# Block inverse read from PSUM at its first turn and turned in storage order at its end, with a replanned order of issue

## The chip, the cores and the metric

One core of one Trainium2 chip runs the whole kernel. The metric is the device time of one execution in microseconds (us). Before the change the median of three executions was 1673.81 us (1667.06 to 1674.06).

## The reference, cut to what matters

The kernel computes two layers on 768 tokens (one sequence of 512, one of 256): a Mamba-2 layer in both directions, then an RWKV-7 layer in both directions, each followed by a residual and a layer norm. The change touches the RWKV-7 recurrence, which for each of 16 heads of 64 channels is

```
def step(s, inp):
    r_t, w_t, k_t, v_t, kk_t, a_t = inp
    sa = einsum('bhvk,bhk->bhv', s, -kk_t)
    s = s * w_t[:, :, None, :] + sa[..., None] * (kk_t * a_t)[:, :, None, :] + v_t[..., None] * k_t[:, :, None, :]
    return s, einsum('bhvk,bhk->bhv', s, r_t)
```

The state s feeds its own update. Taken 64 tokens at a time, all the updates of one chunk solve a unit lower triangular system, and the kernel inverts its 64 by 64 matrix.

## The kernel before, in words

**Stages.** In the Mamba-2 part (0 to about 770 us of the trace) large matmuls, each split into three float32r products (lines 140 to 142), fill TensorE. The RWKV-7 part (from about 770 us) goes over eight blocks b of 128 channels, two heads each. For a block, `rwkv_in` projects and stores the inputs, `p1` prepares six windows of four 64-token chunks, `rwkv_inverse` inverts the 24 units (chunks of both directions), and eight calls of `chain_step` run the recurrence. `rwkv_final` normalises the output. A ring of 32 slots (`slot`, line 697) holds the matrices G, TD and BK of 24 units and of 8 of the next block, so that windows of block b+1 fill slots that steps of block b have freed.

**The windows.** `p1_back` computes a window's matrices into the PSUM tile `ptd` (line 899), which lies in the one buffer of bank tag "s", and VectorE masks them into TD (line 901) and G (line 904, two halves). The last of these reads frees bank "s".

**The inverse.** TD holds a 64 by 64 matrix a unit and head. The two diagonal blocks of 32 by 32 are blended into the SBUF tile TC, laid out as (unit, row), first by ScalarE (line 936) and then by VectorE (line 937), for the first 16 units and then for the other 8. The first turn (line 942, a VectorE transpose of 128x1024) reads TC with the unit innermost, a stride of 32 elements, and writes TS in storage order. Here `sw` swaps the two free dimensions. ScalarE copies TS to the PSUM tile TL, which is taken from bank "s" (line 943); VectorE sets its diagonal (line 944) and solves 30 columns in place, two operations a column (lines 949 and 950). Two turns bring the result to SBUF, both writing at a stride of 32 elements:

```
TL = self.pt("s", [P, 32, 32], "tl")
nc.vector.transpose(TS, sw(TC))
...
nc.vector.transpose(sw(XN), sw(TL))
XR = TC
nc.vector.transpose(sw(XR), TL)
```

The second turn of the end (line 954) reads TL in storage order, the first (line 952) at a stride. Then TL is written again, by matmuls of 32x32 (line 963, TD by XN), so these wait until the turn of line 954 has read it. ScalarE scales the product into E (line 965) and writes XR back to TD (line 968, two operations for each group of units). A second set of 32x32 matmuls (line 972, E by XR) goes to a new tile px, and VectorE and ScalarE copy it to TD (line 975). The steps of the next block wait for that.

**The order of issue.** No order is written by hand. `arrange` (line 1841) gives the whole program to `Program`, whose `estimate` (line 1343) sets the cost of every instruction. `schedule` (line 1768) runs a list scheduler (`forward`, line 1545) under three sets of parameters with eight passes each; `timing` (line 1732) plays every order on a model of the engines (`Machine`, line 1783), and the order with the earliest end becomes a chain of dependences on every engine. SP issues all DMAs, in that order too. In the model a DMA lands DMA_NS = 1700 ns (line 1236) plus its bytes at 250 bytes a ns after its issue, one after another. Three estimates matter later: a VectorE operation of N elements costs (66 + N)/0.96 ns whatever its strides, so a turn is put at 1135 ns; a DMA has no cost for the size of its pieces; and a matmul of another tile size than the one before waits for TURN = 95 ns (line 1240) after the array has drained.

Of the kernel before, what the change touches and what calls it, by code (L numbers as in the profile page):

```python
# [58 lines left out]
class Trunk:  # L59
# [507 lines left out]
    def rwkv(self):  # L567
        nc, d = self.nc, self.d
        with ExitStack() as cx:
# [52 lines left out]
            self.Y = keep(rw, "Y", [NCH, 2, C])  # L622
            ri = self.pool("ri", 1, ctx=tail)
            self.TC, self.TL, self.XN = (keep(ri, n, [32, 32]) for n in ("TC", "TL", "XN"))
            nc.gpsimd.memset(self.TC, 0.0)
            prep = tail.enter_context(ExitStack())
            rp = self.rp = self.pool("rp", 1, ctx=prep)
            self.lora()
# [299 lines left out]
    def rwkv_inverse(self, b):  # L928


        nc = self.nc
        TD, TC, TS, XN = self.TD, self.TC, self.TL, self.XN
        hm = self.halfm
        spans = [(slice(u, u + n), slice(o, o + n)) for u, o, n in self.spans(b)]
        for us, rs in spans:
            nc.scalar.activation(TC[:, us], TD[:, rs, 0, 0:32], AF.Copy, scale=hm[:, 2:3])
            nc.vector.scalar_tensor_tensor(TC[:, us], TD[:, rs, 0, 32:64], hm[:, 3:4], TC[:, us], op0=ALU.mult, op1=ALU.add)
        fl = lambda t: t.rearrange("p a b -> p (a b)")
        sw = lambda t: t.rearrange("p a b -> p b a")

        TL = self.pt("s", [P, 32, 32], "tl")
        nc.vector.transpose(TS, sw(TC))
        nc.scalar.copy(TL, TS)
        nc.vector.memset(fl(TL)[:, ::33], 1.0)
        tmp = fl(XN)
        for j in range(1, 31):
            m = 31 - j
            t = tmp[:, 0 : m * j].rearrange("p (a b) -> p a b", b=j)
            nc.vector.tensor_tensor(t, bc(TS[:, j + 1 : 32, j], 2, j), bc(TL[:, j, 0:j], 1, m), op=ALU.mult)
            nc.vector.tensor_add(TL[:, j + 1 : 32, 0:j], TL[:, j + 1 : 32, 0:j], t)  # L950

        nc.vector.transpose(sw(XN), sw(TL))
        XR = TC
        nc.vector.transpose(sw(XR), TL)
        qs = [(slice(64 * h, 64 * h + 32), slice(64 * h + 32, 64 * h + 64)) for h in range(2)]
        E = TS
        groups = (slice(0, 16), slice(16, 24))
        place = [o + i for _, o, n in self.spans(b) for i in range(n)]
        ps = TL
        for g in groups:  # L960
            for u in range(24)[g]:
                for q0, q1 in qs:
                    nc.tensor.matmul(ps[q1, u, :], TD[q0, place[u], 0, 32:64], XN[q0, u, :], start=True, stop=True)
# [272 lines left out]
DMA_NS = 1700  # L1236
TICK = 10240 / 3
WARM = 2900
SPAN = 3400
TURN = 95.0  # L1240

DRAIN = {"Activation": 122.0, "DVE": 90.0}
FULL = (128, 128)
# [4 lines left out]
        self.keep, self.stay, self.pace, self.spare = keep, stay, pace, spare  # L1248


PASSES = 8
PARAMS = Params(4000, 1000, 1.6, 2.3), Params(6000, 1000, 1.6, 2.0), Params(5000, 2000, 1.6, 2.6)


def size(ap, first=1):
# [24 lines left out]
    return p0 // 32, (p0 + pn + 31) // 32, bits << lo  # L1280


def in_dram(ap):
    lo = int(ap.offset)
    hi = lo + sum((int(n) - 1) * abs(int(s)) for s, n in ap.ap)
    a, z = lo // 4096, hi // 4096
    return 0, 1, ((1 << (z - a + 1)) - 1) << a
# [6 lines left out]
class Program:  # L1294


    def __init__(self, nc, tc):
        self.ins = ins = list(nc.cur_bb.bb.instructions)
        n = len(ins)
        self.eng = [str(x.engine).split(".")[-1] for x in ins]  # L1300
        self.pred = [set() for _ in ins]
        self.cost, self.dma, self.cols = [0.0] * n, [0.0] * n, [0.0] * n
        self.cells, self.kind = [()] * n, [1] * n
        self.mode, self.lock = [FULL] * n, [0.0] * n
        self.part = [None] * n
        self.after, self.rationed = defaultdict(set), set()
        self.raw = set()
        aps, self.acc = [], defaultdict(list)
        for i, x in enumerate(ins):
            io = [[a.bass_ap for a in l if getattr(a, "bass_ap", None) is not None] for l in (x.ins, x.outs)]  # L1310
            aps.append(io)
            for b in io[0] + io[1]:
                if hasattr(b.tensor, "cap_key"):
                    self.acc[b.tensor.name].append(i)
            if io[0] or io[1]:
                self.estimate(i, x, *io)
        self.trace(nc, tc, aps)
        self.classify()
# [24 lines left out]
    def estimate(self, i, x, src, dst):  # L1343
        e, op = self.eng[i], x.opcode
        if e == "SP":
            dram = src and dst and any(hasattr(a.tensor, "cap_key") and space(a.tensor, "DRAM") for a in src + dst)
            self.cost[i] = 1.0 if not dst else 560.0 if dram else 400.0
            if dst:
                self.dma[i] = size(dst[0], 0) * 4 / 250.0
            return  # L1350
        if e == "PE":
            N, M, K = size(src[0]), size(src[1]), int(src[0].ap[0][1])
# [4 lines left out]
            if x.is_transpose:  # L1357
                self.cost[i] = 2 * max(N, M) / 2.4 + 2.5
                self.cols[i] = 2 * N * K / 128
                return  # L1360
            self.mode[i] = up(K), up(M)
            if not f32:
                r = str(x.ins[0].dtype) == "dt.float32r"
                self.cost[i] = N / (2.226 if r else 2.4) + 2.0
                self.cols[i] = N * K / 128
                if N >= 256:
                    self.kind[i] = 2
                    if r and M <= 64:
                        self.mode[i] = FULL
                return  # L1370
# [3 lines left out]
            self.cost[i] = cyc / 2.4 + 2.5  # L1374
            self.cols[i] = (2 if M <= 64 else 4) * N * K / 128
            if M <= 64:
                self.cost[i] = max(N, 64) / 64 * 108.0
                if N < 64:
                    self.cost[i] = 93.0
                self.kind[i] = 0  # L1380
            return
        N = max(size(a) for a in src + dst)
# [6 lines left out]
        if e == "DVE":  # L1389
            if op != "TensorScalarPtr":  # L1390
                c = (66 + N) / 0.96
                if op == "Reciprocal":
                    c = 70 + N * 6.4
            elif x.ins and two == 1 and not ps:
                c = 69 + N / 1.92 + 61 * ptr
            else:
                c = (66 + N) / 0.96 + 61 * ptr
            if getattr(x, "is_tensor_tensor_scan", False):
                c = 70 + 2.07 * N
            if not ps and N > 16:  # L1400
# [4 lines left out]
        elif op == "Memset":  # L1405
            c = 35 + 0.8333 * N
        elif op == "TensorScalarPtr":
            c = 130 + N * 0.83 + 90 * ptr
            self.lock[i] = c - 60
        elif two > 1:  # L1410
            c = 160 + 1.6 * N if N < 200 else 190 + 1.75 * N
            self.lock[i] = c - 60
        else:
            c = 130 + 0.9 * N
            self.lock[i] = c - 60
# [111 lines left out]
    def tails(self):  # L1527
# [6 lines left out]
        todo = [i for i in range(n) if not left[i]]  # L1534
        while todo:
            i = todo.pop()
            tail[i] += self.cost[i] + (DMA_NS + self.dma[i] if self.dma[i] else 0)
# [156 lines left out]
    def backward(self, end):  # L1694
# [21 lines left out]
        for _ in range(n):  # L1716
# [5 lines left out]
                free[e] = t = t + cost[i]  # L1722
            else:
                t = ready[i]
            tail[i] = t + (DMA_NS + self.dma[i] if self.dma[i] else 0)
# [6 lines left out]
    def timing(self, order):  # L1732

        n, eng = len(self.pred), self.eng
        m = Machine(self)
# [6 lines left out]
        for i, s in self.after.items():  # L1742
            left[i] += len(s)
            for j in s:
                asucc[j].append(i)

        def go(i, t):
            end[i] = z = m.run(i, t)
# [19 lines left out]
    def schedule(self, par=None):  # L1768

        best = None  # L1770
        for p in [par] if par else PARAMS:
            prio = [-v for v in self.tails()]
            for _ in range(PASSES):
                order = self.forward(p, prio)
                end = self.timing(order)
                if best is None or max(end) < best[0]:
                    best = max(end), order
                prio = [-v for v in self.backward(end)]
        self.makespan = best[0]
        return best[1]  # L1780


class Machine:


    def __init__(self, p):
        self.p, self.free, self.part = p, defaultdict(float), defaultdict(lambda: None)
        self.mode, self.ring = FULL, 0.0
        self.cell = [0.0] * 16
        self.work, self.held = defaultdict(float), {"DVE": 0.0, "Pool": 0.0}  # L1790

    def run(self, i, t):
# [13 lines left out]
        self.part[e], self.free[e] = p.part[i], end  # L1806
        if p.dma[i]:
            self.ring = max(self.ring, t + DMA_NS) + p.dma[i]
            end = self.ring
        return end  # L1810

    def matmul(self, i, t):
# [3 lines left out]
        c, mode = p.cost[i], p.mode[i]  # L1816
        drained = max(cell)
        if mode != self.mode:
            t = max(t, drained) + TURN
            c += TURN if mode == FULL else 42.0  # L1820
        elif t > drained + 60:
            c += TURN
        else:
            t = max(t, max(cell[q] for q in p.cells[i]))
        self.mode = mode
        start, work = t, p.cols[i]
        c0, k = c, int(t // TICK)
        while c > 1e-9:
# [55 lines left out]
```

## Time and profile before

| | |
|---|---|
| median of three runs | 1673.81 us |
| the profiled execution, its own time | 1676.05 us |
| its span, first to last instruction | 1674.3 us |
| TensorE busy, share of the span | 1521.8 us, 91% |
| VectorE busy | 1372.5 us, 82% |
| ScalarE busy | 840.7 us, 50% |
| GpSimd busy | 756.5 us, 45% |
| mean granted TensorE clock | 0.957 of 2.4 GHz |

PE is TensorE, PEld its weight loads, DVE VectorE, ACT ScalarE, POOL GpSimd, SP the engine that issues DMAs. A busy share is an average over all stages. In a table of stretches, PEclk is the granted clock as a share of 2.4 GHz. In a row of a group, the text behind the bar is its busy time in us, the mean ns of one, and the idle time before it with what ended it. A line that belongs to a helper gathers work of many places, so tiles (pj, TL, px) tell these apart. The matmuls of float32 appear as two records each.

### The profile page before, as it was taken

The page shows a single profiled execution, that of the slowest core. Times are in us where ns is not written, and L with a number is a line of the kernel's source. Part 1 is how long each engine was busy: PE and PEld are TensorE (multiplying, and loading weights), DVE is VectorE, ACT ScalarE, POOL GpSimd, SP SyncE. Part 2 cuts the span into 40 slices and gives each one's busy share as a digit, 9 for nine tenths or more (in the row PEclk, how much of TensorE's full clock was granted, in tenths as well). Part 3 has the DMA queues.
Part 4 walks back from the last instruction along what each step waited for, and adds up shares of the span by engine and source line. Part 5 has one row for each costly group of instructions (what it writes and reads, how often), then busy time and mean ns, then how long its engine had stood idle before and what let it go on. Part 6 is the DMA issues. An engine that isn't in the chain of part 4 may idle for free.

```text
span 1674.3 us, 39379 instructions
## 1 busy us (share of the span) xinstructions
PE 1521.8 (91%) x15210; PEld 1286.0 (77%) x15210; DVE 1372.5 (82%) x3041; ACT 840.7 (50%) x1950; POOL 756.5 (45%) x1026
## 2 busy tenths in 40 slices
PE   7999999999999999998887989989898999978993
PEld 6888888888878799997766767767676767767882
DVE  6779888797887984678698798988898987989578
ACT  4344444545444452314464648565565747565332
POOL 1168356665574460012262628364473727364204
PEclk9999999999999999999998899999999999979996
DMA  5120211221211152602444243443425243363412
GB/s 173 38 63 21 76 63 33 70 83 59 69 35 60 44 180 79 206 39 95 123 134 132 63 113 113 119 123 94 137 84 146 90 123 106 110 200 89 142 50 76
DMA packets 150316, 161.41 MB, mean 96 GB/s; under 512 B 39632, under 2 KB 106928, under 8 KB 150128
## 3 DMA queue, kind: packets, MB, share of 16 engines
q1 hardware_dynamic: 150128, 158.89, 31.3%
q8 instruction: 120, 1.97, 0.5%
q14 instruction: 68, 0.56, 0.1%
HBM read 121.43 MB, written 40.55 MB: 97 GB/s over the span
## 4 chain that ended last, share of the span: by engine, by line
PE 55%; DVE 19%; POOL 10%; DMA 7%; ACT 4%; issue 4%; SPq 1%; DVEq 0%; ACTq 0%; POOLq 0%
PE pj L140 7%; PE pj L142 7%; PE pj L141 7%; PE po L140 3%; PE po L142 3%; PE po L141 3%; POOL G L890 2%; PE pz L140 2%; PE pz L141 2%; PE pz L142 2%; POOL G L888 2%; DMA Wr<-ind 2%; PE pst L380 2%; PE ptd L899 2%; PE py L1025 2%
## 5 line engine op out<-in xcount | busy, mean ns | idle before, releaser
L140 PE MATMUL pj<-xh,whi 128*128 128x512 f32 (+1 forms) x1056 | 379.6, 360 | 18.8 <-ACT whi L122 12.8
L142 PE MATMUL pj<-xh,wlo 128*128 128x256 f32 (+1 forms) x1056 | 374.8, 355 | 3.3 <-DVE wlo L123 3.3
L141 PE MATMUL pj<-xl,whi 128*128 128x512 f32 (+1 forms) x1056 | 373.2, 353 | 0.7 <-DVE xl L136 0.7
L140 PEld LDWEIGHTS pj<-xh,whi 128*128 128x128 f32 x1056 | 204.7, 194 | 46.1 <-ACT whi L122 13.4
L142 PEld LDWEIGHTS pj<-xh,wlo 128*128 128x128 f32 x1056 | 205.0, 194 | 29.5 <-DVE wlo L123 5.8
L141 PEld LDWEIGHTS pj<-xl,whi 128*128 128x128 f32 x1056 | 205.5, 195 | 24.8 <-DVE xl L136 1.7
L122 ACT CAST whi<-wraw 128x512 fp32r<-128x512 f32 x217 | 133.7, 620 | 135.9 <-PE pj L141 59.9
L123 DVE TENSOR_TENSOR wlo<-wraw,whi 128x512 fp32r<-128x512 f32 x217 | 160.4, 744 | 44.9 <-ACT whi L122 43.7
L414 POOL TENSOR_SCALAR G<-past,ddt,dt 128x128 f32<-128x128 f32 x192 | 134.6, 711 | 85.8 <-DVE ddt L320 58.5
L140 PE MATMUL po<-whi,xh 128*128 128x256 f32 x528 | 154.5, 293 | 1.5 <-DVE acc L497 1.5
L142 PE MATMUL po<-whi,xl 128*128 128x256 f32 x528 | 153.7, 291 | 0.0
L141 PE MATMUL po<-wlo,xh 128*128 128x256 f32 x528 | 152.6, 289 | 0.0
L234 DVE SCALAR_TENSOR_TENSOR conv<-conv,convw 128x770 f32<-128x770 f32 x128 | 138.4, 1084 | 1.0
L140 PE MATMUL pz<-whi,xh 128*128 128x256 f32 x384 | 117.0, 305 | 2.0 <-ACT conv L226 1.9
L141 PE MATMUL pz<-wlo,xh 128*128 128x256 f32 x384 | 112.4, 293 | 0.0
L378 POOL TENSOR_TENSOR xw<-xB,dtws 128x256 f32<-128x256 f32 x64 | 51.8, 817 | 133.6 <-ACT xB L366 120.8
L142 PE MATMUL pz<-whi,xl 128*128 128x256 f32 x384 | 112.2, 292 | 0.0
L888 POOL TENSOR_TENSOR G<-EP,Wr 64x256 f32<-64x256 f32 x96 | 89.9, 936 | 42.8 <-DMA Wr<-ind 28.1
L140 PEld LDWEIGHTS po<-whi,xh 128*128 128x128 f32 x528 | 102.5, 194 | 3.4 <-DVE acc L497 1.9
L1039 POOL TENSOR_TENSOR ZP<-SV,PC 64x128 f32<-64x128 f32 x128 | 65.3, 519 | 86.3 <-DVE SV L1051 70.5
L142 PEld LDWEIGHTS po<-whi,xl 128*128 128x128 f32 x528 | 102.4, 194 | 1.8 <-DVE xl L136 0.2
L141 PEld LDWEIGHTS po<-wlo,xh 128*128 128x128 f32 x528 | 102.4, 194 | 0.8 <-DVE wlo L123 0.2
(271 smaller groups left out, 3883.8 us busy)
## 6 DMA issues: line engine op xcount, KB each, us to landing
wraw<-in_r_w_in SPq DMA_DIRECT2D x72, 256.0 KB
Wr<-ind SPq DMA_DIRECT2D x48, 384.0 KB
wraw<-in_m_w_xbc SPq DMA_DIRECT2D x64, 256.0 KB
wraw<-in_m_w_z SPq DMA_DIRECT2D x32, 256.0 KB
wraw<-in_m_w_out SPq DMA_DIRECT2D x32, 256.0 KB
ydram<-yst SPq DMA_DIRECT2D x16, 384.0 KB
yraw<-ydram SPq DMA_DIRECT2D x24, 256.0 KB
ind<-k SPq DMA_DIRECT2D x32, 192.0 KB
```

The source lines that it names most:

```text
L122: nc.scalar.copy(hi, raw)
L123: nc.vector.tensor_sub(lo, raw, hi.bitcast(F32))
L140: mm(ps, ah, bh, start=first, stop=False)
L141: mm(ps, ah, bl, start=False, stop=False)
L142: mm(ps, al, bh, start=False, stop=last)
L234: nc.vector.scalar_tensor_tensor(acc, u[:, t : t + n], w[:, b, t : t + 1], acc, op0=ALU.mult, op1=ALU.add)
L378: nc.gpsimd.tensor_tensor(hv(xw), hv(xB[c][:, 0:256]), bc(self.dtws[:, c, z, hs], 2, 64), op=ALU.mult)
L380: nc.tensor.matmul(ps, xB[c][:, 256:384], xw, start=True, stop=True)
L414: nc.gpsimd.tensor_scalar(G[:, h, :], self.past, self.ddt[:, c, i : i + 1], self.dt[:, c, 0, i : i + 1], op0=ALU.mult, op1=ALU.add)
L888: nc.gpsimd.tensor_tensor(G[hr, ps4, h, 0, :], EP[hr, :, 0:C], w4(tok(W[hr, h])), op=ALU.mult)
L890: nc.gpsimd.tensor_tensor(rho[..., ::-1] if z else rho, EP[hr, :, 1:], w4(tok(W[hr, 2])), op=ALU.mult)
L1039: nc.gpsimd.tensor_tensor(ZP[HR[h], :, s, :], SV[HR[h], :, s, h, :], bc(pc[s][HR[h]], 2, C), op=ALU.mult)
```

## The change

It has two parts. In `rwkv_inverse` the blend goes to PSUM (TL) in place of SBUF (TC), the eight unused units of TL are zeroed there by VectorE in each inverse (in place of one memset of TC on GpSimd at the start), and the first turn reads TL. The turns at the end write XN and XR in storage order. XN and XR are then used through `sw`, that is, the matmuls of lines 963 and 972 and ScalarE's operation of line 968 read them at a stride of 32 elements.

The planner gets other estimates, a landing time of DMAs that grows with the number of their pieces, and another choice among orders: four sets of parameters with ten passes each, each order played once as estimated and three times with random delays added to its DMAs, and the sum of the four ends decides.

```
-            nc.gpsimd.memset(self.TC, 0.0)
...
-        TD, TC, TS, XN = self.TD, self.TC, self.TL, self.XN
+        TD, XR, TS, XN = self.TD, self.TC, self.TL, self.XN
...
-        for us, rs in spans:
-            nc.scalar.activation(TC[:, us], TD[:, rs, 0, 0:32], AF.Copy, scale=hm[:, 2:3])
-            nc.vector.scalar_tensor_tensor(TC[:, us], TD[:, rs, 0, 32:64], hm[:, 3:4], TC[:, us], op0=ALU.mult, op1=ALU.add)
...
         TL = self.pt("s", [P, 32, 32], "tl")
-        nc.vector.transpose(TS, sw(TC))
+        for us, rs in spans:
+            nc.scalar.activation(TL[:, us], TD[:, rs, 0, 0:32], AF.Copy, scale=hm[:, 2:3])
+            nc.vector.scalar_tensor_tensor(TL[:, us], TD[:, rs, 0, 32:64], hm[:, 3:4], TL[:, us], op0=ALU.mult, op1=ALU.add)
+        nc.vector.memset(TL[:, 24:], 0.0)
+        nc.vector.transpose(TS, sw(TL))
         nc.scalar.copy(TL, TS)
...
-        nc.vector.transpose(sw(XN), sw(TL))
-        XR = TC
-        nc.vector.transpose(sw(XR), TL)
+        nc.vector.transpose(XN, sw(TL))
+        nc.vector.transpose(XR, TL)
+        XN, XR = sw(XN), sw(XR)
...
-TURN = 95.0
+TURN = 94.0
...
-PASSES = 8
-PARAMS = Params(4000, 1000, 1.6, 2.3), Params(6000, 1000, 1.6, 2.0), Params(5000, 2000, 1.6, 2.6)
+PASSES, TRIALS, LATE = 10, 4, 800
+PARAMS = Params(8000, 0, 1.6, 2.0), Params(8000, 0, 1.6, 2.6), Params(8000, 1000, 1.4, 2.0), Params(12000, 1000, 1.6, 2.6)
...
+def run(ap):
+
+    n = 1
+    for s, k in reversed(ap.ap[1 if hasattr(ap.tensor, "_space") and not space(ap.tensor, "DRAM") else 0 :]):
+        if k > 1 and s != n:
+            break
+        n *= k
+    return n
...
+                self.late[i] = max(0, n / min(run(a) for a in src + dst) - 128) * 2.3
+                if any(s == 0 and k > 1 for a in src for s, k in a.ap):
+                    self.late[i] += 1100.0
...
-                self.cost[i] = max(N, 64) / 64 * 108.0
-                if N < 64:
-                    self.cost[i] = 93.0
+                self.cost[i], self.extra[i] = (64.5, 20.0) if max(K, M) <= 32 else (116.6 if N <= 64 else N * 1.703, 49.0)
+                self.leave[i] = 100 + 0.82 * N
...
+            if any(N > 64 and len(a.ap) > 1 and abs(int(a.ap[-1][0])) >= 16 and space(a.tensor, "SBUF") for a in src + dst):
+                c += 0.78 * N
...
-            c = 160 + 1.6 * N if N < 200 else 190 + 1.75 * N
+            c = 185 + 1.6 * N if N < 200 else 222 + 1.75 * N
...
+        slip = [chance.expovariate(1 / LATE) if seed and x else 0.0 for x in self.dma]
...
-                if best is None or max(end) < best[0]:
-                    best = max(end), order
+                score = max(end) + sum(max(self.timing(order, s)) for s in range(1, TRIALS))
+                if best is None or score < best[0]:
+                    best = score, order
...
-            t = max(t, drained) + TURN
-            c += TURN if mode == FULL else 42.0
+            t = max(t, drained + TURN if self.mode == FULL else self.gone)
+            c += p.extra[i]
```

## Rows read from the trace of the kernel before

**Rows 1.** The page's busy shares of the engines over the whole span.

```profile
PE 1521.8 (91%) x15210; PEld 1286.0 (77%) x15210; DVE 1372.5 (82%) x3041; ACT 840.7 (50%) x1950; POOL 756.5 (45%) x1026
```

**Rows 2.** Busy times by stretch, first a table of two stretches of the Mamba-2 part, then one of the seven periods of the RWKV-7 part from one first turn to the next, with their sum. Columns: the stretch, its length, then busy us of each engine (instructions), the granted clock, the share of the DMA engines, GB/s.

```profile
50.00:350.00 300.00, 295.48 (x2083) 253.91 (x2082) 247.75 (x465) 138.45 (x300) 167.19 (x203) 1.00 0.17 52
350.00:650.00 300.00, 292.82 (x2210) 255.59 (x2209) 244.43 (x503) 140.99 (x308) 163.10 (x214) 0.99 0.25 77
...
864.70:961.10 96.40, 80.83 (x1000) 65.72 (x999) 77.45 (x170) 54.07 (x130) 41.70 (x63) 0.88 0.37 108
961.10:1052.10 91.00, 83.52 (x1104) 66.48 (x1105) 82.88 (x183) 56.16 (x143) 46.47 (x68) 0.96 0.38 109
1052.10:1148.90 96.80, 86.61 (x1160) 67.20 (x1160) 84.54 (x196) 59.55 (x151) 53.99 (x79) 0.95 0.42 121
1148.90:1241.80 92.90, 83.57 (x1140) 65.45 (x1139) 80.90 (x184) 56.85 (x146) 45.37 (x70) 0.96 0.35 104
1241.80:1334.70 92.90, 82.24 (x1138) 65.66 (x1137) 84.67 (x192) 58.28 (x149) 51.73 (x76) 0.96 0.42 122
1334.70:1429.70 95.00, 86.32 (x1121) 67.53 (x1120) 79.55 (x186) 58.18 (x147) 46.06 (x68) 0.93 0.37 108
1429.70:1522.50 92.80, 79.75 (x1115) 63.54 (x1113) 85.39 (x195) 58.37 (x150) 49.17 (x71) 0.91 0.51 149
sum 657.80, PE 582.84 PEld 461.58 DVE 575.36 ACT 401.45 POOL 334.48; mean PE 83.26 PEld 65.94 DVE 82.19 ACT 57.35 POOL 47.78
```

**Rows 3.** The same for the eight stretches of the inverses alone, from the first turn to about the last: the third of them and the sum of the eight.

```profile
1052.10:1095.30 43.20, 36.74 (x352) 27.55 (x350) 42.09 (x127) 20.91 (x54) 14.70 (x21) 1.00 0.43 120
...
sum 354.25, PE 306.77 PEld 240.22 DVE 335.10 ACT 157.75 POOL 105.96; mean PE 38.35 PEld 30.03 DVE 41.89 ACT 19.72 POOL 13.24
```

**Rows 4.** The groups of the inverse that the change touches, by line, engine and shape.

```profile
L942 DVE STREAM_TRANSPOSE TL<-TC 128x1024 f32<-128x1024 f32 x8 | 16.0, 2004 | 0.0
L952 DVE STREAM_TRANSPOSE XN<-tl 128x1024 f32<-128x1024 f32 x8 | 15.9, 1982 | 0.2
L954 DVE STREAM_TRANSPOSE TC<-tl 128x1024 f32<-128x1024 f32 x8 | 15.5, 1940 | 0.0
L937 DVE SCALAR_TENSOR_TENSOR TC<-TD,halfm,TC 128x512 f32<-128x512 f32 x8 | 6.5, 814 | 0.1
L944 DVE MEMSET tl<- 128x32 f32 x8 | 0.7, 85 | 0.0
L936 ACT ACTIVATE TC<-TD,halfm 128x512 f32<-128x512 f32 x8 | 5.7, 714 | 0.0
L968 ACT ACTIVATE TD<-TC,halfm 128x512 f32<-128x512 f32 x16 | 11.5, 718 | 13.7 <-DVE TC L954 13.7
```

**Rows 5.** Groups of VectorE with an operand in PSUM and all operands in storage order, in two sizes, and one that blends in place with a scalar from a tile, as line 937 does.

```profile
L432 DVE TENSOR_TENSOR yo<-po,eacs 128x256 f32<-128x256 f32 x32 | 13.3, 416 | 3.0 <-PE po L429 2.6 <-POOL yv L436 0.2
L432 DVE TENSOR_TENSOR yo<-po,eacs 128x512 f32<-128x512 f32 x16 | 10.9, 681 | 0.2 <-PE po L429 0.2
L726 DVE SCALAR_TENSOR_TENSOR rv<-pj,hmu,rv 128x511 f32<-128x511 f32 x32 | 23.8, 742 | 3.5 <-ACT rv L724 3.4
```

**Rows 6.** VectorE's instructions in order of time at the start of the third inverse: start in us, length in us, and in brackets the idle time before.

```profile
1049.54 0.69 DVE L901 TENSOR_TENSOR TD<-ptd,maskc 128x512 f32<-128x512 f32 x1 [0.40 <-PE ptd L899]
1050.26 0.69 DVE L904 TENSOR_TENSOR G<-ptd,maskc 64x512 f32<-64x512 f32 x1
1050.99 0.48 DVE L937 SCALAR_TENSOR_TENSOR TC<-TD,halfm,TC 128x256 f32<-128x256 f32 x1
1051.51 0.68 DVE L904 TENSOR_TENSOR G<-ptd,maskc 64x512 f32<-64x512 f32 x1
1052.11 1.93 DVE L942 STREAM_TRANSPOSE TL<-TC 128x1024 f32<-128x1024 f32 x1
```

**Rows 7.** TensorE at the end of the inverses: the groups of the 32x32 matmuls, then, from TensorE's instructions in order of time in the fifth inverse, the first set, a run of others, and the second set.

```profile
L963 PE MATMUL tl<-XN,TD 32*32 32x32 f32 x768 | 18.6, 210 | 11.3 <-DVE TC L954 9.0 <-ACT TL L965 2.3
L972 PE MATMUL px<-TC,TL 32*32 32x32 f32 x768 | 16.3, 203 | 1.8 <-issue 1.0 <-ACT TL L965 0.8
...
1285.33 1.92 PE L963 MATMUL tl<-XN,TD 32*32 32x32 f32 x64 [3.57 <-DVE TC L954]
1292.69 1.71 PE L972 MATMUL px<-TC,TL 32*32 32x32 f32 x96
```

**Rows 8.** Busy times of a stretch just behind that first set, columns as in rows 2.

```profile
1287.30:1290.70 3.40, 3.40 (x15) 3.30 (x16) 1.50 (x2) 2.93 (x6) 0.62 (x1) 0.50 0.86 243
```

**Rows 9.** Transfers on the chain of waits that ended last, in the third period: start in us, time in us, the transfer.

```profile
1058.97 3.01 DMA wur<-in_r_up
1084.48 2.17 DMA rsd<-rows
1087.26 4.19 DMA rb<-rsd
1096.84 4.53 DMA Wr<-ind
```

More of the change, by code (lines that the diff above doesn't have):

```diff
@@ L3 @@
 import math
+import random
 from collections import defaultdict, deque
@@ L1304, in __init__ @@
         self.mode, self.lock = [FULL] * n, [0.0] * n
-        self.part = [None] * n
+        self.part, self.late = [None] * n, [0.0] * n
+        self.extra, self.leave, self.fast = [49.0] * n, [0.0] * n, [False] * n
         self.after, self.rationed = defaultdict(set), set()
@@ L1347, in estimate @@
             self.cost[i] = 1.0 if not dst else 560.0 if dram else 400.0
+            if dram and len(dst[0].ap) > 2:
+                self.cost[i] = 650.0
             if dst:
-                self.dma[i] = size(dst[0], 0) * 4 / 250.0
+                n = size(dst[0], 0)
+                self.dma[i] = n * 4 / 250.0
+                self.late[i] = max(0, n / min(run(a) for a in src + dst) - 128) * 2.3
+                if any(s == 0 and k > 1 for a in src for s, k in a.ap):
+                    self.late[i] += 1100.0
             return
@@ L1359, in estimate @@
                 self.cols[i] = 2 * N * K / 128
+                self.extra[i] = 57.0
                 return
@@ L1362, in estimate @@
             if not f32:
-                r = str(x.ins[0].dtype) == "dt.float32r"
+                r = self.fast[i] = str(x.ins[0].dtype) == "dt.float32r"
+                self.extra[i] = 106.0
                 self.cost[i] = N / (2.226 if r else 2.4) + 2.0
@@ L1536, in tails @@
             i = todo.pop()
-            tail[i] += self.cost[i] + (DMA_NS + self.dma[i] if self.dma[i] else 0)
+            tail[i] += self.cost[i] + (DMA_NS + self.dma[i] + self.late[i] if self.dma[i] else 0)
             for j in self.pred[i]:
@@ L1724, in backward @@
                 t = ready[i]
-            tail[i] = t + (DMA_NS + self.dma[i] if self.dma[i] else 0)
+            tail[i] = t + (DMA_NS + self.dma[i] + self.late[i] if self.dma[i] else 0)
             for j in self.pred[i]:
@@ L1730, in backward, with timing @@
         return tail
-    def timing(self, order):
+    def timing(self, order, seed=0):
         n, eng = len(self.pred), self.eng
@@ L1745, in timing @@
                 asucc[j].append(i)
+        chance = random.Random(seed)
+        slip = [chance.expovariate(1 / LATE) if seed and x else 0.0 for x in self.dma]
         def go(i, t):
-            end[i] = z = m.run(i, t)
+            end[i] = z = m.run(i, t) + slip[i]
             todo = [(j, t) for j in asucc.get(i, ())]
@@ L1775, in schedule @@
                 end = self.timing(order)
-                if best is None or max(end) < best[0]:
-                    best = max(end), order
+                score = max(end) + sum(max(self.timing(order, s)) for s in range(1, TRIALS))
+                if best is None or score < best[0]:
+                    best = score, order
                 prio = [-v for v in self.backward(end)]
-        self.makespan = best[0]
+        self.makespan = best[0] / TRIALS
         return best[1]
@@ L1788, in __init__ @@
         self.mode, self.ring = FULL, 0.0
+        self.fast, self.gone = True, 0.0
         self.cell = [0.0] * 16
@@ L1808, in run @@
             self.ring = max(self.ring, t + DMA_NS) + p.dma[i]
-            end = self.ring
+            end = self.ring + p.late[i]
         return end
@@ L1818, in matmul @@
         if mode != self.mode:
-            t = max(t, drained) + TURN
-            c += TURN if mode == FULL else 42.0
+            t = max(t, drained + TURN if self.mode == FULL else self.gone)
+            c += p.extra[i]
         elif t > drained + 60:
-            c += TURN
+            c += p.extra[i]
         else:
-            t = max(t, max(cell[q] for q in p.cells[i]))
-        self.mode = mode
+            t = max(t, max(cell[q] for q in p.cells[i]) - (81 if p.fast[i] and not self.fast else 0))
+        self.mode, self.fast, self.gone = mode, p.fast[i], max(self.gone, t + p.leave[i])
         start, work = t, p.cols[i]
```

## The prediction

> **What bounds the kernel now.** The sum is made against the profiled execution's own time, 1676.05 us: its span of 1674.3 us and 1.75 us around it. The median of the three runs, 1673.81, lies 2.2 us below. A measurement of this kernel tells about 0.5% from no change, 8.4 us: faster means below 1665.4, slower above 1682.2.
>
> I read the page's shares first: TensorE 91% busy, VectorE 82% [rows 1]. An average hides the stages, so the stretches come next. In the Mamba-2 part TensorE is busy for 588.3 of 600 us (98%) at the full granted clock [rows 2]; no order of issue has much to win there, and I put the change at nothing there, because TensorE's own work covers whatever moves on the others. In the seven whole periods of the RWKV-7 part both engines are near their ends and neither is full: TensorE is busy 582.8 of 657.8 us (88.6%), VectorE 575.4 (87.5%) [rows 2]. The mean period is 94.0 us, the shortest 91.0 and the longest 96.8. The granted clock is below 1 in every one of them; a PEclk of 0.88 over 96.4 us means about 23 us at the lower of the two levels, 1.2 GHz.
>
> Inside a period the inverses stand out: in their eight stretches, 354.3 us in all, VectorE is busy 335.1 us, 94.6%, TensorE 86.6%, ScalarE 44.5% [rows 3]. There VectorE sets the pace. The period is also a loop: a step of block b frees slots, windows of block b+1 fill them, the inverse of b+1 needs the last window, and the steps of b+1 need the inverse. So time saved on VectorE inside an inverse can shorten the period, eight times.
>
> **The change, part by part.**
>
> *The three turns.* They take 2.004, 1.982 and 1.940 us for 1024 elements [rows 4]. VectorE with an operand in PSUM and every operand in storage order takes 0.681 us for 512 elements and 0.416 for 256 [rows 5], so 0.265 for each 256 more and, as an estimate, 0.681 + 2 x 0.265 = 1.21 us for 1024. All three turns have a side in SBUF at a stride, and each costs 0.73 to 0.79 us over that estimate, 0.77 ns an element. Afterwards none has. Two still read PSUM at a stride. Does that cost anything? The trace bounds it: the turn of line 952 has both a strided read of PSUM and a strided write of SBUF and costs only 0.04 us more than that of line 954 with the strided write alone [rows 4]. Either the read is nearly free, or it costs as much and runs beside the write. I take it as free, the value nearest to those 0.04, and keep 2.0 us for these two turns as the other end. Gain: 0.79 + 0.77 + 0.73 = 2.29 us an inverse, 0.73 at the other end.
>
> Beside it a rule. The Trainium skill ("SBUF — State Buffer", section "Door 1: The DMA port swizzle") says that strided access pays for each new 16-byte line in SBUF, and that PSUM's lines are only 8 bytes, so that non-contiguous access there costs matmuls dearly. The price of a strided SBUF side agrees with rows 4; by the second half the two PSUM reads would stay slow, and the gain would be 0.73 us an inverse. No row here shows that half alone; it is the third case below.
>
> *The zeroing of the eight units.* Between 0.085 us (32 elements, line 944 [rows 4]) and 0.416 (256 elements of another operation [rows 5]); I take 0.085 + 224 x 1.035 ns = 0.32 us of VectorE an inverse. The memset that goes from GpSimd ran once, on an engine 45% busy: nothing.
>
> *The blend.* Line 937 takes 0.814 us for 512 elements in SBUF; the same kind of blend with PSUM takes 0.742 [rows 4, 5]. Nothing, with -0.07 as the other end.
>
> So VectorE loses 2.29 - 0.32 = 1.97 us an inverse, 15.8 us over eight.
>
> *A new wait.* The blend now writes bank "s", which the last window's ptd holds until VectorE has read it for the last time. Before, the 16-unit part of the blend ran ahead, into SBUF; only the 8-unit part was left, squeezed between the last masks, and the first turn began as soon as the last mask ended. From the end of that mask (1052.19) to the end of the turn (1054.04) passed 1.85 us [rows 6]. Now the whole blend queues behind the mask: 0.71 on ScalarE (its 256-element part then runs beside VectorE), 0.74 and 0.48 on VectorE, the turn 1.21, some 0.1 of handing over: 3.24 us. What waits behind it on VectorE in that gap is other work of the block, which the planner can put there; what waits for it is the copy of line 943 and the solve. So the delay of the inverse grows by 1.4 us at its start and falls by 1.5 at its end, where the 32x32 matmuls wait for both turns. By delay alone the inverse is worth nothing; by VectorE's work it is worth 15.8 us. With VectorE at 94.6% I go nearer to the second end: **-10 us**.
>
> At the end of the inverse there is something to win beyond delay. TensorE stood idle for 9.0 us before the first set of matmuls, waiting for the turn of line 954, once for 3.57 us [rows 7]; just behind that wait the granted clock was 0.50, that is 1.2 GHz, for a stretch of 3.4 us in which TensorE was busy throughout [rows 8]. I count this inside the -10.
>
> *Strided reads by ScalarE.* Line 968 reads XR at a stride. At 0.77 ns an element, VectorE's price, its 512-element form (0.718 us [rows 4]) grows by 0.39 and the 256-element form by 0.20; two of each make 1.2 us an inverse, 9.4 in all. ScalarE is 44.5% busy in these stretches [rows 3], and the operation can go behind line 965, which alone feeds the second set. Nothing, with +9.4 if the cover is gone.
>
> *Strided reads by TensorE.* The 32x32 matmuls of both sets now read 32 columns at a stride. No row shows such a read. The nearest is again 0.77 ns an element, 25 ns a record; 96 records take 1.71 us, 18 ns each [rows 7]. With 1536 records the upper end is +38 us. A gain is excluded, since nothing is taken away. I take nothing: records that overlap tenfold, 203 ns long every 18 ns [rows 7], have room for a slower read.
>
> *The order of issue.* The trace of before cannot show an order that does not exist yet, so I bound it by periods that it does show. If all seven went like the shortest, 7 x 3 = 21 us would go; if all went like the longest, 7 x 2.8 = 20 would come [rows 2]. What speaks for a gain is how wrong the old estimates were: a turn was put at 1.14 us and took 2.0; the DMA rb was put at 1.7 + 0.79 = 2.49 us and took 4.19, Wr at 3.27 and took 4.53, rsd at 1.72 and took 2.17 [rows 4, 9]. The three DMAs make 3.4 us a period that the planner did not see, on its chain, 24 us over seven. The mended formula gives rb 3.59 and Wr 3.86, nearer. What speaks against is that an order chosen for the sum of four playings, three with random delays, gives up some of the end as estimated; and another order moves every engine's queue, SP's DMAs with it, in a stage where TensorE has only 11% to spare. I take a quarter of the 24: **-6 us**.
>
> **Sum:** 1676.05 - 10 - 6 = 1660.
>
> **The rivals.**
>
> 1. *The order gives more.* All of VectorE's 15.8 and periods like the shortest: 1676 - 15.8 - 21 = 1639. For it: the clock is below 1 in all seven periods [rows 2], and a drop costs twice the time of what runs in it. Against: the shortest period is one of seven.
> 2. *The order gets worse (the slower side).* The new order puts idle gaps of TensorE where the old one had dense work, the clock drops behind them, and periods go like the longest: 1676 - 10 + 20 = 1686. The place is the handover between windows, inverse and steps; the point from which it decides is a mean period above 94.0 + 10/7 = 95.4 us, where it eats the inverse's gain. For it: the period with a granted clock of 0.88 is among the longest [rows 2], so one more such drop a period is enough.
> 3. *The inverse gives nothing.* Strided PSUM reads keep two turns at 2.0 us, so that 0.73 - 0.32 = 0.41 us an inverse is left (3.3 in all), or the wait for bank "s" takes the rest; the order is neutral: 1673. For it: the sum of delays above. Against: VectorE's 94.6%.
> 4. *Strided reads slow the matmuls.* 1660 + 38 = 1698; from about 15 ns a record it makes the kernel slower.
>
> **How the numbers follow.** The forecast (1650 to 1668) has 0.48, rival 1 has 0.15, rival 2 0.12, rival 3 0.20, rival 4 0.05. Of the forecast's share 0.03 lies above 1665.4. Faster: 0.45 + 0.15 = 0.60; the same: 0.03 + 0.20 = 0.23; slower: 0.12 + 0.05 = 0.17. The range reaches to rival 1 and to rival 2 and leaves out rival 4 and the far tails: 1636 to 1686. The likeliest case's own range is 1650 to 1668.
>
> **What the profile after would show.** Right: the three turns at 1.1 to 1.3 us; the new memset at about 0.3; the inverses' stretches with about 2 us less of VectorE each; periods of 92 to 93 us. The first turn should follow the last mask by about 2 us, with other work of VectorE between. Wrong: turns of lines 942 and 952 near 2.0 us (rival 3); 96 records of 32x32 matmuls in clearly over 1.7 us at the full clock (rival 4); periods above 95.4 us with a lower granted clock (rival 2); or a saving that lies in the Mamba-2 part, where I put none.

## The result and the profile after

The kernel after takes 1650.49 us (median of four runs, 1647.05 to 1652.36) against 1673.21 of the kernel before, also of four. The ratio is 0.987, with a 95% interval of 0.984 to 0.990: faster by 1.3%, about 22 us. The forecast was 1660 in a range of 1636 to 1686, and the likeliest case's own range, 1650 to 1668, holds it at its edge. Every ratio here and below is to the kernel before, run beside the other; over all these runs the kernel before scatters from 1664 to 1685 us by itself, so a difference of a few us says little.

The profiled execution spans 1648.9 us, 25.4 less than before. Two marks split this, the starts of the first and of the eighth first turn (the turn that opens an inverse). The first inverse's first turn starts at 857.1 us (864.7 before): 7.6 us. From the first to the eighth first turn pass 640.5 us (657.8): 17.3 us. What follows takes 151.3 us (151.8): 0.5 us.

Busy times by stretch of the kernel after, in the columns of [rows 2]: two stretches of the Mamba-2 part, then the first and the last of the seven periods and the sum of the seven.

```profile
50.00:350.00 300.00, 298.07 (x2115) 254.50 (x2114) 253.44 (x472) 142.56 (x308) 165.06 (x208) 1.00 0.16 52
350.00:650.00 300.00, 294.81 (x2258) 260.57 (x2258) 246.89 (x514) 138.02 (x304) 154.59 (x209) 0.99 0.26 81
...
857.10:944.00 86.90, 82.19 (x1069) 67.78 (x1067) 77.94 (x171) 54.84 (x134) 37.04 (x61) 0.94 0.39 111
...
1405.20:1497.60 92.40, 76.97 (x1085) 63.37 (x1084) 82.40 (x190) 58.44 (x146) 46.63 (x66) 0.89 0.48 140
sum 640.50, PE 589.17 PEld 472.74 DVE 571.19 ACT 409.77 POOL 327.19; mean PE 84.17 PEld 67.53 DVE 81.60 ACT 58.54 POOL 46.74
```

The mean period is 91.5 us (94.0 before); the first, which had the lowest granted clock before (0.88 over 96.4 us), now has 0.94 over 86.9, while the last has 0.89. Read the counts in brackets in the Mamba-2 rows: in the same 300 us TensorE works on 2115 matmul records where it had 2083, and on 2258 where it had 2210 [rows 2]. Its idle time in these 600 us falls from 11.7 to 7.1 us. The busy share, 98% before and 99% now, hardly shows either.

The groups of the inverse, which answer to [rows 4] and, for the last two, to [rows 7]. Lines 943, 953 and 954 are the three turns, 941 and 940 the blend, 942 the new zeroing, 969 ScalarE's writing of XR, 964 and 973 the two sets of 32x32 matmuls.

```profile
L943 DVE STREAM_TRANSPOSE TL<-tl 128x1024 f32<-128x1024 f32 x8 | 9.9, 1240 | 0.1
L953 DVE STREAM_TRANSPOSE XN<-tl 128x1024 f32<-128x1024 f32 x8 | 10.0, 1249 | 0.2
L954 DVE STREAM_TRANSPOSE TC<-tl 128x1024 f32<-128x1024 f32 x8 | 9.7, 1211 | 0.0
L941 DVE SCALAR_TENSOR_TENSOR tl<-TD,halfm,tl 128x512 f32<-128x512 f32 x8 | 6.0, 747 | 0.5 <-ACT tl L940 0.5
L942 DVE MEMSET tl<- 128x256 f32 x8 | 2.2, 272 | 0.9
L940 ACT ACTIVATE tl<-TD,halfm 128x512 f32<-128x512 f32 x8 | 5.5, 692 | 8.3 <-DVE G L904 8.3
L969 ACT ACTIVATE TD<-TC,halfm 128x512 f32<-128x512 f32 x16 | 19.4, 1213 | 8.3 <-DVE TC L954 8.3
L964 PE MATMUL tl<-XN,TD 32*32 32x32 f32 x768 | 24.6, 228 | 10.2 <-DVE TC L954 10.2
L973 PE MATMUL px<-TC,TL 32*32 32x32 f32 x768 | 23.2, 228 | 1.5 <-ACT TL L966 1.5
```

The eight stretches of the inverses alone, as in [rows 3], sum to:

```profile
sum 323.60, PE 286.03 PEld 231.63 DVE 302.82 ACT 153.75 POOL 69.02; mean PE 35.75 PEld 28.95 DVE 37.85 ACT 19.22 POOL 8.63
```

They are 30.7 us shorter and hold 32.3 us less of VectorE's work, 4.0 us each, while the seven periods lose 17.3 us. The turns explain 17.8 us of that work; the rest is work that the new order does elsewhere in the period.

The turns fall from about 2.0 us to 1.21 to 1.25, the two that read PSUM at a stride among them. Against that stand ScalarE's line 969, which grows from 0.718 to 1.213 us, and the two sets of matmuls, whose busy time grows from 18.6 and 16.3 us to 24.6 and 23.2. In ScalarE's row of line 940 the new wait shows: 8.3 us of idle time, ended by the last mask (line 904).

The second set in TensorE's instructions in order of time, in the fifth inverse (start in us, length, line); [rows 7] has 1.71 us for it. Below it stand a stretch around the set of before and one around this set, in the columns of [rows 2]: both ran at the full granted clock.

```profile
1270.70 2.89 PE L973 MATMUL px<-TC,TL 32*32 32x32 f32 x96
...
1292.60:1294.50 1.90, 1.90 (x99) 1.77 (x98) 1.90 (x2) 0.38 (x1) 1.82 (x3) 1.00 0.72 232
...
1270.60:1273.70 3.10, 3.10 (x98) 2.91 (x98) 1.27 (x2) 2.13 (x6) 3.02 (x4) 1.00 0.47 132
```

VectorE at the start of the third inverse, which answers to [rows 6]: from the last mask to the first turn, other work of the planner's choice left out.

```profile
1029.98 0.68 DVE L904 TENSOR_TENSOR G<-ptd,maskc 64x512 f32<-64x512 f32 x1
...
1031.17 0.94 DVE L826 SCALAR_TENSOR_TENSOR gth<-gth,g 128x768 f32<-128x768 f32 x1
1032.04 0.74 DVE L941 SCALAR_TENSOR_TENSOR tl<-TD,halfm,tl 128x512 f32<-128x512 f32 x1
...
1035.08 1.24 DVE L943 STREAM_TRANSPOSE TL<-tl 128x1024 f32<-128x1024 f32 x1
```

5.7 us pass from the end of the mask to the end of the turn (4.4 to its start), where 1.85 passed before, but VectorE is not idle in them: the gap is filled, by line 826 and others.

### The profile page after: what moved, and what is told of

Its sections match the earlier page's. It is cut to its first block, busy times and chain, and to the rows that moved or that the text cites. A ratio compares the mean times of both kernels' runs of the same rounds, so it can differ in the third digit from the quotient of the medians.

```text
span 1648.9 us, 39430 instructions
## 1 busy us (share of the span) xinstructions
PE 1522.4 (92%) x15210; PEld 1291.4 (78%) x15210; DVE 1369.1 (83%) x3049; ACT 847.0 (51%) x1950; POOL 740.4 (45%) x1025
## 5 line engine op out<-in xcount | busy, mean ns | idle before, releaser
L143 PE MATMUL pj<-xh,wlo 128*128 128x512 f32 (+1 forms) x1056 | 373.1, 353 | 2.1 <-DVE wlo L124 1.7
L124 DVE TENSOR_TENSOR wlo<-wraw,whi 128x512 fp32r<-128x512 f32 x217 | 164.9, 765 | 36.7 <-ACT whi L123 35.5
L415 POOL TENSOR_SCALAR G<-past,ddt,dt 128x128 f32<-128x128 f32 x192 | 126.2, 667 | 80.0 <-DVE ddt L321 55.9
L888 POOL TENSOR_TENSOR G<-EP,Wr 64x256 f32<-64x256 f32 x96 | 82.7, 862 | 51.2 <-DMA Wr<-ind 28.4
```

Source lines behind the costliest of these rows:

```text
L124: nc.vector.tensor_sub(lo, raw, hi.bitcast(F32))
L143: mm(ps, al, bh, start=False, stop=last)
L415: nc.gpsimd.tensor_scalar(G[:, h, :], self.past, self.ddt[:, c, i : i + 1], self.dt[:, c, 0, i : i + 1], op0=ALU.mult, op1=ALU.add)
L888: nc.gpsimd.tensor_tensor(G[hr, ps4, h, 0, :], EP[hr, :, 0:C], w4(tok(W[hr, h])), op=ALU.mult)
```

## The experiments

The change has two parts, and a new program always gets a new order, so taking a part away changes everything else too. The experiments therefore come in two kinds: four where the planner made a new order, and eight where an order was written into the kernel as a list and not planned (a pinned order).

**The inverse alone, old planner.** The new `rwkv_inverse` in the kernel before.

> The new inverse under the old planner, whose order is made anew for it. Theory A (both parts add): VectorE is freed of about 2 us an inverse and some 10 to 16 us of the 23 us appear here, 1657 to 1663 us. Rival B (the order of issue is everything; any new order lands somewhere by luck): no relation to the inverse, anywhere from 1655 to 1690. Rival C (the inverse is everything): 1648 to 1653.

1669.85 us, ratio 0.9963 (0.994 to 0.9985): 6 us, less than Theory A asked for.

**The planner alone, old inverse.** The old `rwkv_inverse` in the kernel after.

> The old inverse under the new planner (new estimates, landing times, trials, parameters). Theory A: the rest of the gain, 7 to 13 us, so 1660 to 1666, and the first first-turn of the trace starts about 7 us earlier than the 864.7 us of before. Rival B: anywhere from 1645 to 1690. Rival C: 1670 to 1676.

1674.77 us, ratio 0.9986 (0.9958 to 1.0015): nothing that can be told from no change. The first first-turn starts at 864.9 us, not 7 us earlier. A and C both fall, C because it asked 1648 to 1653 of the inverse alone: the parts alone give 6 and 2 us, together 22. Either an order's worth is luck, or each part needs the other.

**New estimates, old choice.**

```
-PASSES, TRIALS, LATE = 10, 4, 800
+PASSES, TRIALS, LATE = 8, 1, 800
-PARAMS = Params(8000, 0, 1.6, 2.0), Params(8000, 0, 1.6, 2.6), ...
+PARAMS = Params(4000, 1000, 1.6, 2.3), Params(6000, 1000, 1.6, 2.0), ...
```

> The kernel after with its new estimates and landing times, but the old choice among orders: the three old parameter sets, eight passes, no trials with random delays. Theory A, estimates matter and the choice does not: 1648 to 1656. Rival: the choice (trials and parameters) brings the order's share: 1658 to 1668.

1659.68 us, ratio 0.9897 (0.9854 to 0.9941). It misses the first theory's 1656 by 4 us and lies in the rival's range; the interval reaches both. The estimates with the new inverse carry most of the gain; the new choice carries a smaller part, not clear of noise.

**Other seeds for the trials.** `range(1, TRIALS)` became `range(11, 10 + TRIALS)`.

> The kernel after with three other seeds for the random delays of the trials, so that another of the 40 candidate orders may win. If the choice is robust, 1647 to 1654. If the order is luck, it lands 6 us or more away on either side. It shows how far one order lies from another at equal estimates.

1649.7 us, ratio 0.9843 (0.9803 to 0.9884). This trace and that of after start the same instructions in the same order on every engine, but for a few neighbours that swap places, as they do in the pinned copy of that order below. So the same order won again, and this is a repeat of after. It says that the choice holds against three other seeds; how far one order lies from another it cannot say.

**Does the planner's ranking hold on the chip?** Two of the 40 orders that the new planner makes for the kernel after, pinned: the one that it ranks second, close behind its choice, and one far behind.

> The kernel after with the order that the new planner scores second best of its 40, 0.1% behind its choice in the planner's own sum. If the planner's ranking holds on the chip: 1645 to 1656. If orders of like score scatter by luck: 1657 to 1675.

1655.09 us, ratio 0.9887 (0.9855 to 0.992).

> The kernel after with an order that the planner scores 2.2% behind its choice (the seventh pass of the third parameter set). If the ranking holds: 1675 to 1695. If the score says little: 1650 to 1670.

1684.03 us, ratio 1.0055 (1.0034 to 1.0077): slower than the kernel before, with the same instructions as after. On these two the ranking holds, though not its spacing: 0.1% of the planner's sum came out as some 0.3% against the base below, at the edge of the forecast. Between the best order and a poor one lie some 34 us by the ratios and 37 by the medians, more than the whole gain of the change. In the poor one 21 of them have arisen by the first first-turn, at 878.5 us.

**The base: the order of after written down.**

> The kernel after with its order of issue written down in place of being planned. Nothing else is changed: 1647 to 1653 on any theory. It is the base for the pinned kernels on the same chip.

1646.52 us, ratio 0.9853 (0.9821 to 0.9886). The kernels below that use this order are read against this one.

**The order of after, all turns as before.**

```
-            nc.scalar.activation(TL[:, us], TD[:, rs, 0, 0:32], AF.Copy, scale=hm[:, 2:3])
+            nc.scalar.activation(XR[:, us], TD[:, rs, 0, 0:32], AF.Copy, scale=hm[:, 2:3])
...
-        nc.vector.transpose(TS, sw(TL))
+        nc.vector.transpose(TS, sw(XR))
...
-        nc.vector.transpose(XN, sw(TL))
-        nc.vector.transpose(XR, TL)
-        XN, XR = sw(XN), sw(XR)
+        nc.vector.transpose(sw(XN), sw(TL))
+        nc.vector.transpose(sw(XR), TL)
```

> The order of after kept instruction for instruction, with the blend and all three turns as before (SBUF at a stride; the zeroing stays on VectorE). Direct theory, VectorE's 2.3 us an inverse stand on the loop of a period: +14 to +20 us over the pinned after. Rival, the order holds the gain and the turns hide in it: 0 to +5. In between if part of the saved work is hidden: +6 to +13.

1655.22 us, ratio 0.989 (0.9859 to 0.992): 8.7 us over the base by the medians, 6 by the ratios, and the intervals overlap a little. So of 18 us of VectorE's work a third to a half reaches the end, as far as six runs can tell. The blend, though back in SBUF, keeps its late place in the order of after. The first first-turn starts at 858.4 us, and the seven periods sum to (columns as in [rows 2]):

```profile
sum 644.80, PE 583.70 PEld 466.77 DVE 585.11 ACT 399.46 POOL 323.68; mean PE 83.39 PEld 66.68 DVE 83.59 ACT 57.07 POOL 46.24
```

With the old turns the order of after thus takes 13.0 us off the periods of before; with the new ones they come to 640.5 in after and to 633.7 in the base, in the fastest of its executions.

**The order of after, only the two end turns as before** (the last part of that diff).

> The order of after kept, with only the two turns at the end as before. The old blend and all old turns together cost 0.989 to 0.985 of before, some 6 to 9 us. If the end turns carry it (two of three turns, and TensorE waits for them): +4 to +9 over 1646.5. If the first turn does: 0 to +3.

1651.03 us, ratio 0.9855 (0.9825 to 0.9886): 4.5 us by the medians, nothing by the ratios. The end turns are not shown to pay at all. The groups of the 32x32 matmuls in this kernel, columns as above (its line numbers are one lower):

```profile
L963 PE MATMUL tl<-XN,TD 32*32 32x32 f32 x768 | 19.3, 213 | 20.5 <-DVE TC L954 20.5
L972 PE MATMUL px<-TC,TL 32*32 32x32 f32 x768 | 16.8, 208 | 1.8 <-ACT TL L965 1.8
```

With operands in storage order they are back at 19.3 and 16.8 us, where the base has 24.5 and 23.2, while TensorE's idle time before the first set doubles from 10.4 to 20.5 us. So 10 us more of waiting stand against 12 us less in the matmuls: the turns cost TensorE time either way, before the matmuls if they are slow, in the matmuls if they are fast.

**The order of before, only the two end turns as after.**

> The order of before kept instruction for instruction, with only the two turns at the end of the inverse written in storage order (blend and first turn stay in SBUF, so no new wait for bank s). If the turns help in any order: 8 x 1.5 us of VectorE's work, of which half shows, 1664 to 1669. If they help only in an order planned for them: 1671 to 1675. If strided operands of the 32x32 matmuls and of ScalarE cost more than the turns save: over 1676.

1670.2 us, ratio 0.9977 (0.9951 to 1.0004): 3 to 4 us, at the edge of what can be told from nothing, as in the other order.

**The order of before, the whole new inverse.** The blends move behind the last mask, as bank "s" demands.

> The order of before kept, with the new inverse; only the blends move behind the last mask, since bank s is held until then. Direct theory: 1655 to 1662. If the wait for the bank eats the gain, as the sum of delays says: 1668 to 1677. A planned order for the same inverse under the old planner gave 0.996 of before.

1691.51 us, ratio 1.0113 (1.0076 to 1.0151): 19 us slower, worse than either theory had it. VectorE at the start of its third inverse in order of time, then ScalarE's two parts of the blend:

```profile
1056.98 1.39 DVE L904 TENSOR_TENSOR G<-ptd,maskc 64x512 f32<-64x512 f32 x2
1059.13 0.76 DVE L941 SCALAR_TENSOR_TENSOR tl<-TD,halfm,tl 128x512 f32<-128x512 f32 x1 [0.76 <-ACT tl L940]
1060.43 0.49 DVE L941 SCALAR_TENSOR_TENSOR tl<-TD,halfm,tl 128x256 f32<-128x256 f32 x1 [0.55 <-ACT tl L940]
...
1061.35 1.25 DVE L943 STREAM_TRANSPOSE TL<-tl 128x1024 f32<-128x1024 f32 x1
...
1058.40 0.69 ACT L940 ACTIVATE tl<-TD,halfm 128x512 f32<-128x512 f32 x1 [1.37 <-DVE G L904]
1059.92 0.48 ACT L940 ACTIVATE tl<-TD,halfm 128x256 f32<-128x256 f32 x1 [0.82 <-DVE tl L941]
```

Here the gap behind the mask is not filled: VectorE waits for ScalarE's blend, 0.76 and 0.55 us in this inverse (9.9 us over all eight), and its whole queue behind it. ScalarE's second part does not run beside VectorE but waits for its first blend, so that from the end of the mask to the end of the turn 4.2 us pass, where 1.85 passed before. The sum of its seven periods, columns as in [rows 2]:

```profile
sum 674.10, PE 605.79 PEld 482.52 DVE 567.41 ACT 411.35 POOL 334.29; mean PE 86.54 PEld 68.93 DVE 81.06 ACT 58.76 POOL 47.76
```

96.3 us a period: VectorE has 8 us less work than before and the periods are 16 us longer. The end turns alone gained 3 to 4 us in this order, so the loss comes with the move of blend and first turn to PSUM, at the place that the blends were given here. A planned order, in the first experiment, made 6 us of gain out of the same inverse.

**The order of after, the Mamba-2 part in the order of before.** On every engine the places of the Mamba-2 instructions are filled with the same instructions in their old sequence.

> The kernel after, with the instructions of the Mamba-2 part put back into the order of before on every engine and the RWKV-7 part in the order of after. If the 7 us by which the first inverse starts earlier in after come from the order of the Mamba-2 part, 1655 to 1659. If that lead would be waited away later, or comes from the RWKV-7 part's first projections: 1649 to 1653.

1661.58 us, ratio 0.993 (0.9903 to 0.9958): 13 (ratios) to 15 us (medians) over the base, the intervals are apart, and it is more than the first theory asked for. The first first-turn starts at 870.0 us against 856.6 in the base. Its Mamba-2 stretches, columns as before:

```profile
50.00:350.00 300.00, 295.08 (x2075) 252.97 (x2074) 247.30 (x464) 137.78 (x297) 167.12 (x202) 1.00 0.16 52
350.00:650.00 300.00, 292.67 (x2190) 255.76 (x2189) 244.51 (x503) 139.65 (x307) 163.59 (x214) 0.98 0.25 78
```

The counts fall back to 2075 and 2190, those of the kernel before nearly, and its periods sum to 641.6 us, after's 640.5 nearly (633.7 in the base, whose profiled execution is the fastest of its six). So the lead of the Mamba-2 part comes from its order and is not waited away later. How large it is depends on the trace of before that one takes. With the Mamba-2 part in the order of before the first first-turn starts at 864.7 us in the kernel before, but at 869.8, 869.8 and 870.0 in the three pinned kernels with that order; in the order of after it starts at 856.6 to 858.4 in five traces. That is 6 to 13 us, and the 7.6 us of the two main profiles stand near its lower end. The seam between the two orders adds nothing that shows at this mark, since the two kernels wholly in the order of before have 869.8 as well.

## Why the prediction was right, and which of its steps were not

**Right: the direction, and the total of the periods.** The periods were to lose 16 us in all (-10 for the inverse, -6 for the order); they lost 17.3 by the two profiles, and a mean of 92 to 93 us was named where 91.5 came. That the total fits is in part luck: by the pinned kernels the split was nearer 4 to 11 for the inverse and 13 for the order, and two costs that were put at nothing stand inside it. The time fell 10 us below the forecast mainly because of a part that the sum left out, the Mamba-2 part.

**The turns.** Forecast 1.21 us each, measured 1.24, 1.25 and 1.21. The third rival's first half, strided PSUM reads that stay slow, is out: they cost 0.03 to 0.04 us over the turn that reads in order. By the Trainium skill's rule on PSUM's short lines ("SBUF — State Buffer", section "Door 1: The DMA port swizzle"), carried over to VectorE, lines 943 and 953 would have stayed near 2.0; for VectorE the trace does not agree. The zeroing was put at 0.32 and takes 0.272 us; the blend, put at nothing, fell from 0.814 to 0.747. VectorE was to do about 2 us less in each stretch of an inverse; it does 4.0 us less, since the new order also moved other work out.

**The wait for bank "s".** It came, and the planner put other work of VectorE in its gap, but it is longer than forecast. 3.24 us were named from the mask to the end of the turn; 4.2 pass in the pinned order of before, because ScalarE's second blend waits for VectorE where I had it run beside, and 5.7 in after, with other work between. The first turn was to follow the mask by about 2 us and follows by 4.4. What I did not see is how much hangs on the filling: in an order without it the new inverse costs 19 us. The forecast priced this wait at nothing beyond delay; the step was mis-sized for any order not made for it.

**Strided reads by TensorE: the term taken as nothing was 12.9 us.** The two sets' busy time went from 34.9 to 47.8 us over eight inverses, 8.4 ns a record, between my bounds of 0 and 25. The step that failed is "records that overlap tenfold ... have room for a slower read": 96 records take 2.89 us in place of 1.71, both at the full granted clock. From start to start a record in storage order takes 16 ns at the full granted clock and 27 ns at 1.2 GHz, a strided one 28 ns at either. So at the full clock the price is 12 ns, and 8.4 is the mean over both levels. The fourth rival's mechanism is real; its price lies below the 15 ns from which I had it make the kernel slower.

**Strided reads by ScalarE: 11.6 us of its time, where 9.4 was the upper end.** Line 968 took 11.5 us for its larger form and 8.0 for its smaller, together 19.5; line 969 takes 31.1. The estimate by VectorE's 0.77 ns an element was low: 0.495 us more on 512 elements is 0.97 ns. (VectorE's own price, by the turns before and after, is 0.71 to 0.75 ns; the prediction's 0.77 is the upper of its three differences.) Whether it was covered, as the forecast assumed, no run separates.

**The inverse's -10.** Undone in the order of after it is worth 6 to 9 us. VectorE was freed of 17.8 us by the turns, less 2.2 by the zeroing, and the forecast had 15.8. At the end turns the gain meets its costs: in the order of after the fast turns save TensorE 10 us of idle time before the first set and cost it 12 us in the two sets, and the kernel with the old end turns is not clearly slower. That ScalarE's 11.6 us cost anything at the end is not shown. From the kernel before to the kernel after this idle time hardly fell (11.3 us to 10.2), so the gain beyond delay that I saw there is not to be seen between these two.

**Failed: nothing in the Mamba-2 part.** "TensorE is busy for 588.3 of 600 us ...; no order of issue has much to win there" was the wrong step, and the term was put at nothing. The same 4701 matmul records, up to the last store of the Mamba-2 result, end at 664.5 us in place of 673.8. With this part's order alone put back, the kernel loses 13 to 15 us; by the marks of the traces the part is worth 6 to 13. That is between a quarter and over half of the whole gain. The row that I read already left room: 98% of 600 us leaves 11.7 us idle, more than the 9.3 us won, and 4.6 of them went. Up to that store the idle time fell from 23.2 to 17.4 us in all, 1.4 of it ahead of the first matmul. The rest of the lead lies inside the busy time, which does not tell how densely records follow: from the start of each matmul record of the tile pz to the start of the next pass 160.6 us in all before and 150.1 after, of which only 3.1 us before and none after were idle. The weight loads showed more room: 509.5 of 600 us (85%) in [rows 2], now 515.1. The Trainium skill ("Trainium Kernel Development and Optimization", section "Performance Expectations") says that matmul busy time is a bad measure of distance to the limit since matmuls are pipelined, and the busy share of LDWEIGHTS a good one. On the first half the trace agrees; on the second it shows no more than that a share of 85% still rose.

**The order's -6.** With the old turns, the order of after still takes 1655.2 against 1672.8 us: 17.5 us, so the term was mis-sized. How they divide is not settled: 13 to 15 us for the Mamba-2 part would leave 2.5 to 4.5 for the RWKV-7 part, while the marks give the first 6.3 us and the seven periods 13.0. The first rival's periods, all like the shortest of before (91.0), nearly came, but with a part of the inverse's gain in them. The bounds by good and bad periods were sound in kind: orders of the same program measured from 1646.5 to 1684.0.

**Open.** Which estimate made the order better was not separated: not the landing times of DMAs from the costs of matmuls and VectorE. So my reading that DMAs unseen by the planner cost 24 us is neither shown nor refuted. Why the new planner found nothing for the old inverse is also open: its order there ended the Mamba-2 part at 669.1 us, half of the gain, and had lost it again by the first inverse. An order that does far better with the old turns exists, the pinned order of after at 1655.2 us, so the 2 us of that experiment tell of the order that the planner chose and not of what the old inverse allows; how much of after's order was a lucky find is open too. The clock was not separated either. Over the seven periods the granted clock rose from 0.935 to 0.952; as an estimate, twice the share missing from 1 is the time at 1.2 GHz, 85 us before and 62 after. Whether the periods are shorter because of that or the clock higher because the work is denser, no run tells.

## What to carry to other kernels

A change of operations and a change of order can only be told apart with the order pinned: write down the order of one kernel and run the other's operations in it. Where an engine is "98% busy" with pipelined work, turn the share into idle us, and count instructions in equal stretches, before calling it full. And when a stride is taken from a writer, price it at every reader that gets it.

## What the runs showed that was not expected

A 32x32 float32 matmul whose moving operand has a stride of 32 elements takes 28 ns a record, start to start, in every kernel that has it, whether the granted clock is 2.4 or 1.2 GHz. In storage order it takes 16 ns at 2.4 GHz and 27 at 1.2, so the stride costs most where the clock is high. A VectorE transpose of 1024 elements takes 1.25 us from PSUM at a stride and 1.21 in order, but 1.9 to 2.0 with a strided side in SBUF. One wait for a PSUM bank, 1.3 us of idle VectorE in the inverse shown, went with 2.3 us more a period when the order was not made for it.
